# Seams of a two-layer flow-matching backbone: bank order, earlier loads of z's rows, later scaling of rows

## The chip, the cores and the metric

The kernel runs on one core of one Trainium2 chip. The metric is the device time of one execution in microseconds (us). Three runs of the kernel before took 1910.47, 1912.56 and 1915.56, median 1912.56. One more execution was profiled; it took 1914.06, with a span of 1912.3 from its first to its last instruction.

## The reference

Two layers over 512 latent tokens x with a context of 256 tokens, all of width 2048. Each layer normalises its input, scales and shifts it by vectors made from the conditioning (adaLN), mixes the tokens, normalises again, and adds the gated result to the stream.

```python
for i in range(DEPTH):                                   # 2: a pooling layer, then an attention layer
    shift, scale, gate = split(silu(c) @ ada_w[i] + ada_b[i], 3)
    h_lat = rms_norm(x, pre_norm[i]) * (1 + scale) + shift       # the same for the context with c_ctx
    if is_pool:
        u, g = split(h @ w_in, 2)                        # 2048 -> 2 x 2048
        p = centred_multiscale_pool(u)                   # windows 2, 4, 8, 16; minus the token itself
        p = einsum(p, w_grp) + b_grp                     # 4 groups of 512
        y = (p * scale_ * silu(g)) @ w_out               # z = p * scale_ * silu(g); 2048 -> 2048
    else:
        y = mla_branch(h_lat, h_ctx, ...)                # latent attention, 16 heads
    x = x + gate * rms_norm(y, post_norm[i])             # layer 0 also updates the context
return x
```

## The kernel before, in words

Every large product is split for precision: the activation and the weight each consist of a high and a low part, and mm3 (L197) runs three matmuls, L198, L199 and L200, for one product. Weights come in pieces of 128 x 1024: SP's queue loads raw (L186), ScalarE casts the high part whi (L188), VectorE subtracts to get the low part wlo (L189). Two raw and four split buffers rotate. The results stand in eight banks of 512 columns each. pair() alternates between two latent pairs of banks, 0 and 1 or 2 and 3; context results stand in banks 4 and 5. pss() turns between banks 6 and 7, which hold transposes. hss() is bank 7 alone. bank(kind, ...) hands out banks in rotation.

Each engine works through its own list in order. The lists are put in order by a scheduler from the program below; the yields and steps in the program only say which work is issued beside which weight piece. A wait of the first instruction of a list therefore holds up all that stands behind it.

The stages, in the order of time:

- Opening. ada0 makes the scale of layer 0 (rows_, 4 rows in bank 6). part(kts) then turns four of these rows at a time into columns (scales, transposes L371, small VectorE steps up to L387), transposes four column tiles of x through hss() (make_h0: L280, ScalarE L281, VectorE L282), and multiplies each with the first two pairs of w_in's columns, `first` and `second`. rms_rows (L321) makes the row factors of the first norm: it fills ar with the factor of each token (L331), transposes it through hss() (L334) and copies it to R (L335), which has one factor per column, since the products of this stage have channels on the partitions and tokens along the columns. It is called in the last part, before the last lat_part of `second`. ub are two buffers with pads of zeros, in which u_in (L597) puts the scaled products and from which u_out builds the pooled windows.
- Pool layer, first matmul. gemm1 runs pairs j = 2 to 15 of w_in's columns: j below 8 is u, from 8 on the gate. Each takes four pieces (k4) with 16 row tiles. After each piece after(k4) issues other work: fill() gives out steps of ada_part, the conditioning of the later layers as weighted sums on VectorE (L521). At the last pair, j = 15, after(1) and after(2) call load_z for k2 = 0 and 1, that is for four rows of z. Each gate pair ends with its evacuation: VectorE scales by R (L696), ScalarE applies SiLU, VectorE multiplies with y, and GpSimd's queue writes z1d in device memory (L700).
- load_z (L492) reads two rows of z1d back (L496), scales them and splits them into the activation tiles aL (latent) and cbig (context): ScalarE L499, VectorE L500. The first four rows go through the buffer s2, two of them, which also hold y's rows; the other twelve through xt, three of them.
- Pool layer, last matmul for the latents: products(0), four groups of 512 columns, eight pieces each, four latent tiles, one bank per tile and group by bank("l", 1, 8), which starts at bank 0. z_ahead(k2) loads rows 2(k2 + 2) and the next one while the first group runs. Each group is evacuated with a square for the norm (ScalarE L750) and a product with the gate (VectorE L751), into y.
- The same for the context: products(1), with the groups in the order 3, 0, 1, 2 and banks psb() (six, two per group). late=2 lets evacuation lag by two groups. Its tiles y take the place of the latent ones. Beside each piece lat_post(step) moves the latent rows on: residual (L775) takes the norm, adds x (L782), stores to x1d (L785), and scales the rows for the next norm (L794); it is a generator, and every step advances it twice. make_h (L213) then makes the activation of layer 1: four transposes (L220) into a pss() bank, ScalarE L222, a cast L223, VectorE L224. It is done for two row tiles per step, at steps 16 to 23; steps 24 to 31 are those of the fourth context group.
- The attention layer, and its output groups with the last norm: square (L1214), product with the gate (L1215), factor (rms_r, L202: two small VectorE steps L206 and L208, then a power on GpSimd, L210), four final additions (L1245) and stores.

Of the kernel before, what the change touches and what calls it, by code (L numbers as in the profile page):

```python
# [80 lines left out]
def hybrid_kernel(  # L81
# [206 lines left out]
    with pool("start") as sp:  # L288
# [149 lines left out]
        def part(kts):  # L438
# [3 lines left out]
            yield  # L442
            last = kts[-1] == KT - 1
            for i, kt in enumerate((*kts, None)):
                if kt is not None:
                    c_, o = kt // 4, slice(kt % 4 * P, (kt % 4 + 1) * P)
                    make_h0([xs[c_][:, t, o] for t in range(NTL)], kt, 0)
                    yield
                    make_h0([xs[c_][:, t, o] for t in range(NTL, NT)], kt, 1)
                    yield  # L450
                if i >= 1:
                    piece, k = pieces[(i - 1) // 2], kts[i - 1]
                    lat_part(first, piece, k)
                    if not last:
                        cxt_part(first, piece, k)
                    yield
                    if not last:
                        lat_part(second, piece, k)
                    cxt_part(second, piece, k)
                    if last:  # L460
                        cxt_part(first, piece, k)
                    yield
            if last:
                rms_rows()
                for i, kt in enumerate(kts):
                    lat_part(second, pieces[i // 2], kt)
# [101 lines left out]
    with pool("pa") as ap:  # L568
# [25 lines left out]
        for u in ub:  # L594
            nc.gpsimd.memset(u, 0.0)

# [70 lines left out]
        for j in range(2, 2 * NP):  # L667
# [4 lines left out]
            def after(k4):  # L672
                if j <= NP and k4 < 2:
                    u_out((j - 1) // 2, k4, pieces[(j - 1) // 2])
                if j < 2 * NP - 1:
                    fill(1.6 if j < NP else 2.1)
                if j == 2 * NP - 1 and k4 in (1, 2):
                    load_z(lambda: ap.tile([P, ULEN], F32, name="s2", tag="s2", bufs=2), k4 - 1)

# [51 lines left out]
    with pool("pb") as bp:  # L731
# [3 lines left out]
        def h_of():  # L735
            return adp.tile([P, 1024], F32, name="araw", tag="araw", bufs=2)[:, 0:SEQ]

        def products(v, tiles, act_of, before, order, kept, late=0):

# [13 lines left out]
            for n, cc in enumerate(order):  # L753
                waiting.append((cc, gemm_rows(tiles, act_of, pool_w_out[0], cc, before(n), kept if cc == 3 else None,
                                              psb if v else lambda: bank("l", 1, 8))))
                while len(waiting) > (late if n < 3 else 0):
# [18 lines left out]
        def residual(v, t, y, ssq):  # L775
# [13 lines left out]
            r = rms_r(sq, 2, D)  # L789
            yield  # L790
            for half in range(2):
# [5 lines left out]
        def z_ahead(k2):  # L797
            if k2 + 2 < KT // 2:
                load_z(lambda: bp.tile([P, 1024], F32, name="xt", tag="xt", bufs=XTS), k2 + 2)

# [8 lines left out]

        sums_at = lambda: banks[:, (turns["l"] + 3) % 8 * 512:][:, 0:512]  # L810
        ys, ssq = products(0, range(NTL), actl, ahead, (0, 1, 2, 3), kept)
        lat_res = [residual(0, t, ys[t], ssq[t]) for t in range(NTL)]

        def lat_post(step):
            if step >= 20 and len(halves) <= 2 * NTC:
                x_ahead()
            for t in range(NTL):
                if step >= 4 * t:
                    next(lat_res[t], None)
                    next(lat_res[t], None)  # L820
            for kt in range(2 * (step - 16), 2 * (step - 15)):
                if 0 <= kt < KT:
                    make_h(h_of, ys, kt, 1, 0, nc.scalar.copy if kt % 2 else None)
# [369 lines left out]
    with pool("zr_", "right") as zp, pool("pe") as ep:  # L1193
# [15 lines left out]
        for cc in range(4):  # L1209
# [3 lines left out]
            def evac(t, ps):  # L1213
                nc.scalar.activation(junk[:, 0:512], ps, AF.Square, accum_out=ssq[t][:, cc:cc + 1])  # L1214
                nc.vector.tensor_mul(ys[t][:, cc * 512:(cc + 1) * 512], ps, gp)  # L1215

            if cc < 3:
                for t, ps in enumerate(gemm_rows(range(NTL), zzt, wo, cc, load_z2 if cc == 0 else None)):
                    evac(t, ps)
            else:  # L1220
# [14 lines left out]
                for t in range(NTL):  # L1235
# [3 lines left out]
                    for kt in range(KT):  # L1239
                        mm3(ps, zzt(kt, t * P, P), wt(hold[kt // 2], kt % 2, 0, 512), kt == 0, kt == KT - 1)  # L1240
                    evac(t, ps)
                    r = rms_r(ssq[t], 4, D)
                    for q in range(4):
# [28 lines left out]
```

## Time and profile before

| | |
|---|---|
| median of three runs | 1912.56 us (1910.47 to 1915.56) |
| profiled execution | 1914.06 us, of which span 1912.3 |
| busy: TensorE / VectorE / ScalarE / GpSimd | 98% / 64% / 34% / 6% |
| mean granted clock of TensorE | 0.996 of 2.4 GHz |
| 100 to 120: TensorE busy, granted clock | 17.45 of 20 us, 1.00 |
| 120 to 140 | 17.40, 1.00 |
| 680 to 700 | 16.93, 1.00 |
| 700 to 720 | 15.77, 0.91 |
| 880 to 900 | 17.14, 0.91 |
| 940 to 960 | 20.00, 1.00 |

The stretches are counted from the start of the span. TensorE counts as busy while a matmul is in its pipeline, so a stretch at a lower granted clock can be fully busy and still do less. The granted clock is a share of full speed, 1.00 for 2.4 GHz and 0.50 for 1.2 GHz; values between are means over a stretch. In the rows further below, DVE is VectorE, ACT ScalarE, POOL GpSimd, PE TensorE, and SPq the queue of SyncE. In square brackets stands how long an engine was idle before the instruction, and what ended that.

### The profile page before, as it was taken

The numbers are of one execution on the slowest core, as the hardware profiler recorded it, in microseconds if no ns is written. First come the engines' busy times: TensorE is split into PE (matmuls) and PEld (weight loads), VectorE is DVE, ScalarE is ACT, GpSimd is POOL, SyncE is SP. The second block draws the span as 40 slices with busy tenths as digits, with TensorE's granted clock in tenths as the row PEclk, the third lists the DMA queues.
The fourth block names the chain that finished last, engine by engine and source line by source line (L and its number), as shares of the span: only waits on it lengthen the run. The fifth ranks groups of instructions, "written<-read, shape, count | busy, mean of one in ns | idle before, by whom it ended". The sixth has DMA issues, their size and how long they took to land.

```text
span 1912.3 us, 26140 instructions
## 1 busy us (share of the span) xinstructions
PE 1868.5 (98%) x10496; PEld 1618.4 (85%) x10496; DVE 1214.7 (64%) x1572; ACT 643.3 (34%) x1018; POOL 109.3 (6%) x196
## 2 busy tenths in 40 slices
PE   7989999999999989999999999999999999999998
PEld 6778888888888878887889988789999999998886
DVE  6649696885887786575864255635666666664333
ACT  6722121221211234223743232224444444444230
POOL 0000000000100000002010002200000000000000
PEclk9999999999999999999999999999999999999999
DMA  9825454556776676475751237842111112126334
GB/s 312 278 75 179 151 197 134 178 169 197 230 245 214 231 249 226 154 231 208 240 159 50 76 93 266 287 140 91 50 45 50 56 50 67 50 68 189 103 127 154
DMA packets 170442, 299.75 MB, mean 157 GB/s; under 512 B 19624, under 2 KB 89536, under 8 KB 169808
## 3 DMA queue, kind: packets, MB, share of 16 engines
q1 hardware_dynamic: 155136, 243.84, 40.0%
q0 software_dynamic: 13872, 52.07, 7.7%
q10 hardware_dynamic: 1312, 2.16, 0.3%
q8 instruction: 82, 1.34, 0.3%
q14 instruction: 40, 0.33, 0.1%
HBM read 268.65 MB, written 29.38 MB: 156 GB/s over the span
## 4 chain that ended last, share of the span: by engine, by line
PE 83%; DMA 8%; DVE 4%; issue 2%; ACT 2%; POOL 0%; SPq 0%; DVEq 0%; POOLq 0%; ACTq 0%
PE banks L198 25%; PE banks L199 25%; PE banks L200 25%; DMA garaw<-in_ada_w 3%; PE banks L1155 2%; DMA araw<-in_ada_w 1%; PE banks L1134 1%; PE banks L1135 1%; DVE acc L521 1%; DVE wlo L189 1%; PE banks L145 1%; DMA xs<-in_x 1%; DMA raw<-in_ada_w 1%; PE banks L220 1%; DMA s<-z1d 1%
## 5 line engine op out<-in xcount | busy, mean ns | idle before, releaser
L188 ACT CAST whi<-raw 128x1024 fp32r<-128x1024 f32 (+1 forms) x268 | 274.8, 1027 | 670.1 <-PE banks L199 311.0
L189 DVE TENSOR_TENSOR wlo<-raw,whi 128x1024 fp32r<-128x1024 f32 (+1 forms) x268 | 318.8, 1194 | 283.9 <-ACT whi L188 283.0
L521 DVE SCALAR_TENSOR_TENSOR acc<-araw,sc,acc 128x1024 f32<-128x1024 f32 x240 | 297.9, 1280 | 49.4 <-DMA araw<-in_ada_w 48.7
L198 PE MATMUL banks<-aL,whi 128*128 128x512 f32 x704 | 278.1, 395 | 3.5 <-DVE ub L600 2.6
L200 PE MATMUL banks<-aL,wlo 128*128 128x512 f32 x704 | 276.8, 393 | 2.0 <-DVE wlo L189 2.0
L199 PE MATMUL banks<-aL,whi 128*128 128x512 f32 x704 | 276.7, 393 | 0.0
L198 PE MATMUL banks<-whi,aL 128*128 128x512 f32 (+1 forms) x448 | 164.4, 367 | 7.3 <-ACT aL L499 4.2
L198 PE MATMUL banks<-cbig,whi 128*128 128x256 f32 (+2 forms) x576 | 169.8, 295 | 0.9 <-DVE sg L696 0.9
L199 PE MATMUL banks<-cbig,whi 128*128 128x256 f32 (+2 forms) x576 | 170.3, 296 | 0.0
L200 PE MATMUL banks<-cbig,wlo 128*128 128x256 f32 (+2 forms) x576 | 169.1, 293 | 0.0
L199 PE MATMUL banks<-wlo,aL 128*128 128x512 f32 (+1 forms) x448 | 163.7, 365 | 0.0
L200 PE MATMUL banks<-whi,aL 128*128 128x512 f32 (+1 forms) x448 | 162.6, 364 | 0.0
L200 PEld LDWEIGHTS banks<-aL,wlo 128*128 128x128 f32 x704 | 132.6, 188 | 31.7 <-DVE wlo L189 2.9
L198 PEld LDWEIGHTS banks<-aL,whi 128*128 128x128 f32 x704 | 132.8, 189 | 18.0 <-DVE ub L600 3.0
L199 PEld LDWEIGHTS banks<-aL,whi 128*128 128x128 f32 x704 | 133.1, 189 | 13.9
L199 PE MATMUL banks<-wlo,cbig 128*128 128x256 f32 (+2 forms) x384 | 123.6, 322 | 2.9 <-DVE wlo L189 2.9
L198 PE MATMUL banks<-whi,cbig 128*128 128x256 f32 (+2 forms) x384 | 125.1, 326 | 0.1
L198 PEld LDWEIGHTS banks<-cbig,whi 128*128 128x128 f32 x576 | 108.2, 188 | 19.2 <-DVE sg L696 1.2
L200 PE MATMUL banks<-whi,cbig 128*128 128x256 f32 (+2 forms) x384 | 123.6, 322 | 0.0
L199 PEld LDWEIGHTS banks<-cbig,whi 128*128 128x128 f32 x576 | 108.3, 188 | 17.3
L200 PEld LDWEIGHTS banks<-cbig,wlo 128*128 128x128 f32 x576 | 109.3, 190 | 2.9
L1141 ACT ACTIVATE pr<-banks,nm 128x768 f32<-128x768 f32 x64 | 57.8, 903 | 134.1 <-DVE nm L1138 133.9
(258 smaller groups left out, 3567.7 us busy)
## 6 DMA issues: line engine op xcount, KB each, us to landing
araw<-in_ada_w SPq DMA_DIRECT2D x128, 512.0 KB, 4.3
raw<-in_pool_w_in SPq DMA_DIRECT2D x64, 512.0 KB, 4.7
raw<-in_pool_w_out SPq DMA_DIRECT2D x60, 512.0 KB, 5.2
raw<-in_mla_w_in SPq DMA_DIRECT2D x40, 512.0 KB, 4.2
raw<-in_ada_w SPq DMA_DIRECT2D x32, 512.0 KB, 5.8
garaw<-in_ada_w POOLq DMA_DIRECT2D x32, 512.0 KB, 5.5
raw<-in_mla_w_out SPq DMA_DIRECT2D x32, 512.0 KB, 3.9
raw<-in_mla_w_ukv SPq DMA_DIRECT2D x32, 256.0 KB, 3.1
```

The costliest lines, as they stand in the source:

```text
L145: nc.tensor.transpose(pt[:, k * P:(k + 1) * P], acc[:, (lo + k) * P:(lo + k + 1) * P], ident)
L188: nc.scalar.copy(hi[:, :n], raw[:, :n])
L189: nc.vector.tensor_sub(lo[:, :n], raw[:, :n], f32(hi[:, :n]))
L198: nc.tensor.matmul(o, l[0], r[0], start=start, stop=False)
L199: nc.tensor.matmul(o, l[0], r[1], start=False, stop=False)
L200: nc.tensor.matmul(o, l[1], r[0], start=False, stop=stop)
L220: nc.tensor.transpose(pt[:, t * P:(t + 1) * P], xt[:, kt * P:(kt + 1) * P], ident)
L521: nc.vector.scalar_tensor_tensor(acc[v], raw, w, acc[v], ALU.mult, ALU.add)
L1134: nc.tensor.matmul(to, qr[:, o], krh[:, ks], start=True, stop=False)
L1135: nc.tensor.matmul(to, qr[:, o], krl[:, ks], start=False, stop=False)
L1141: nc.scalar.activation(pr, ps[:, 0:KEYS], AF.Exp, bias=nm, accum_out=zs)
L1155: nc.tensor.transpose(pt[:, t * P:(t + 1) * P], pr[:, t * P:(t + 1) * P], ident)
```

## The change

Six edits, at places that lie far apart in the program.

- rms_rows() is called at the start of the last part, behind its scales and the load of its pieces, and no longer near its end.
- ub's tiles are no longer filled whole by GpSimd; VectorE fills the three stretches of pads of each tile.
- In the last gate pair, after(1), after(2) and after(3) load two pairs of z's rows each, twelve rows in all. z_ahead loads the last four, in the first output group.
- Output groups of the latents take banks from a list: the lat pair that the last gate pair did not use, banks 6 and 7, the pair that it used, banks 4 and 5. The sums of the conditioning that still run there use the bank three turns ahead, as before.
- residual yields six times instead of once before it scales the latent rows. make_h follows at steps 18 to 25.
- At the very end the factor's VectorE steps are issued ahead of the last product.

```diff
--- before.py
+++ after.py
@@ -441,6 +441,8 @@
             pieces = [head_piece(kt) for kt in kts[::2]]
             yield
             last = kts[-1] == KT - 1
+            if last:
+                rms_rows()
             for i, kt in enumerate((*kts, None)):
                 if kt is not None:
                     c_, o = kt // 4, slice(kt % 4 * P, (kt % 4 + 1) * P)
@@ -461,7 +463,6 @@
                         cxt_part(first, piece, k)
                     yield
             if last:
-                rms_rows()
                 for i, kt in enumerate(kts):
                     lat_part(second, pieces[i // 2], kt)
 
@@ -592,7 +593,8 @@
 
         ub = [ap.tile([P, ULEN], F32, name=f"ub{k}") for k in range(2)]
         for u in ub:
-            nc.gpsimd.memset(u, 0.0)
+            for lo, n in ((0, PAD), (PAD + SEQ, 2 * PAD), (3 * PAD + KEYS, ULEN - 3 * PAD - KEYS)):
+                nc.vector.memset(u[:, lo:lo + n], 0.0)
 
         def u_in(ps):
             for m, u in enumerate(ub):
@@ -674,8 +676,9 @@
                     u_out((j - 1) // 2, k4, pieces[(j - 1) // 2])
                 if j < 2 * NP - 1:
                     fill(1.6 if j < NP else 2.1)
-                if j == 2 * NP - 1 and k4 in (1, 2):
-                    load_z(lambda: ap.tile([P, ULEN], F32, name="s2", tag="s2", bufs=2), k4 - 1)
+                if j == 2 * NP - 1 and k4:
+                    for k2 in (2 * k4 - 2, 2 * k4 - 1):
+                        load_z(lambda: ap.tile([P, ULEN], F32, name="s2", tag="s2", bufs=2), k2)
 
             ps = gemm1(j * 2 * P, WAYS if j < NP else GATES, after)
             if j < NP:
@@ -735,6 +738,16 @@
         def h_of():
             return adp.tile([P, 1024], F32, name="araw", tag="araw", bufs=2)[:, 0:SEQ]
 
+
+        free = [2 * (1 - ps), 2 * (1 - ps) + 1, 6, 7, 2 * ps, 2 * ps + 1, 4, 5]
+
+        def lbank(ahead=None):
+            i = turns.get("l", 0)
+            if ahead is None:
+                turns["l"] = i + 1
+            at = free[(i + (ahead or 0)) % 8] * 512
+            return banks[:, at:at + 512]
+
         def products(v, tiles, act_of, before, order, kept, late=0):
 
             ys = []
@@ -752,7 +765,7 @@
 
             for n, cc in enumerate(order):
                 waiting.append((cc, gemm_rows(tiles, act_of, pool_w_out[0], cc, before(n), kept if cc == 3 else None,
-                                              psb if v else lambda: bank("l", 1, 8))))
+                                              psb if v else lbank)))
                 while len(waiting) > (late if n < 3 else 0):
                     evac(*waiting.pop(0))
             return ys, ssq
@@ -787,7 +800,8 @@
                     x_ahead()
                 yield
             r = rms_r(sq, 2, D)
-            yield
+            for _ in range(1 if v else 6):
+                yield
             for half in range(2):
                 o = slice(half * 1024, (half + 1) * 1024)
                 with tc.high_priority(offset=-50):
@@ -795,8 +809,8 @@
                 yield
 
         def z_ahead(k2):
-            if k2 + 2 < KT // 2:
-                load_z(lambda: bp.tile([P, 1024], F32, name="xt", tag="xt", bufs=XTS), k2 + 2)
+            if k2 + 6 < KT // 2:
+                load_z(lambda: bp.tile([P, 1024], F32, name="xt", tag="xt", bufs=XTS), k2 + 6)
 
         def ahead(n):
             def step(k2):
@@ -807,7 +821,7 @@
 
         kept = {}
 
-        sums_at = lambda: banks[:, (turns["l"] + 3) % 8 * 512:][:, 0:512]
+        sums_at = lambda: lbank(3)
         ys, ssq = products(0, range(NTL), actl, ahead, (0, 1, 2, 3), kept)
         lat_res = [residual(0, t, ys[t], ssq[t]) for t in range(NTL)]
 
@@ -818,7 +832,7 @@
                 if step >= 4 * t:
                     next(lat_res[t], None)
                     next(lat_res[t], None)
-            for kt in range(2 * (step - 16), 2 * (step - 15)):
+            for kt in range(2 * (step - 18), 2 * (step - 17)):
                 if 0 <= kt < KT:
                     make_h(h_of, ys, kt, 1, 0, nc.scalar.copy if kt % 2 else None)
 
@@ -1212,7 +1226,9 @@
 
             def evac(t, ps):
                 nc.scalar.activation(junk[:, 0:512], ps, AF.Square, accum_out=ssq[t][:, cc:cc + 1])
+                r = rms_r(ssq[t], 4, D) if cc == 3 else None
                 nc.vector.tensor_mul(ys[t][:, cc * 512:(cc + 1) * 512], ps, gp)
+                return r
 
             if cc < 3:
                 for t, ps in enumerate(gemm_rows(range(NTL), zzt, wo, cc, load_z2 if cc == 0 else None)):
@@ -1238,8 +1254,7 @@
                     ps = psb()
                     for kt in range(KT):
                         mm3(ps, zzt(kt, t * P, P), wt(hold[kt // 2], kt % 2, 0, 512), kt == 0, kt == KT - 1)
-                    evac(t, ps)
-                    r = rms_r(ssq[t], 4, D)
+                    r = evac(t, ps)
                     for q in range(4):
                         o = slice(q * 512, (q + 1) * 512)
                         nc.vector.scalar_tensor_tensor(ys[t][:, o], ys[t][:, o], r, xt[:, o], ALU.mult, ALU.add)
```

On TensorE, at the start of the last part of the opening (hwh are weights; xs is x, ar the row factors), before:

```order
L371 MATMUL banks<-ident,ar 128x4 [waits Activation_49]
L371 MATMUL banks<-ident,ar 128x4 x3
L280 MATMUL banks<-ident,xs 128x128 [waits DMAHW6_49,Activation_49]
L280 MATMUL banks<-ident,xs 128x128 x3
L198 MATMUL banks<-aL_103,hwh 128x512 [waits Activation_49]
L198 MATMUL banks<-aL_103,hwh 128x512 x3
L280 MATMUL banks<-ident,xs 128x128 [waits DMAHW7_49,DVE_49]
L280 MATMUL banks<-ident,xs 128x128
```

and now:

```order
L371 MATMUL banks<-ident,ar 128x4 [waits Activation_49]
L371 MATMUL banks<-ident,ar 128x4 x3
L334 MATMUL banks<-ident,ar 128x128 [waits DVE_49,Activation_49]
L334 MATMUL banks<-ident,ar 128x128 x3
L334 MATMUL banks<-ident,ar 128x128 [waits DVE_49]
L334 MATMUL banks<-ident,ar 128x128
L280 MATMUL banks<-ident,xs 128x128 [waits DMAHW6_49,DVE_49]
L280 MATMUL banks<-ident,xs 128x128 x3
L198 MATMUL banks<-aL_103,hwh 128x512 [waits Activation_49]
```

Six transposes of ar stand between the transposes of the scales and those of xs; before, they stand behind the last products of this part.

On VectorE, in the second context group, around the scaling of the first rows of y, before:

```order
L782 SCALAR_TENSOR_TENSOR y<-y,r,xt 128x1024 [waits Pool_49]
L782 SCALAR_TENSOR_TENSOR y<-y,r,xt 128x1024 [waits DMAHW3_49]
L794 TENSOR_SCALAR y<-y,r 128x1024 [waits DMASW5_49]
L794 TENSOR_SCALAR y<-y,r 128x1024 [waits DMASW6_49]
L189 TENSOR_TENSOR wlo<-raw,whi 128x1024 [waits DMAHW0_49,Activation_49]
L206 TENSOR_REDUCE ms<-sq 128x1 [waits Activation_49]
L189 TENSOR_TENSOR wlo<-raw,whi 128x1024 [waits DMAHW1_49,PE_49]
L208 TENSOR_SCALAR ms<-ms 128x1 [waits DVE_49]
L189 TENSOR_TENSOR wlo<-raw,whi 128x1024 [waits DMAHW2_49,Activation_49]
```

and now, where L782 has become L795 and L794 has become L808:

```order
L795 SCALAR_TENSOR_TENSOR y<-y,r,xt 128x1024 [waits Pool_49]
L795 SCALAR_TENSOR_TENSOR y<-y,r,xt 128x1024 [waits DMAHW3_49]
L189 TENSOR_TENSOR wlo<-raw,whi 128x1024 [waits DMAHW0_49,Activation_49]
L189 TENSOR_TENSOR wlo<-raw,whi 128x1024 [waits DMAHW1_49,Activation_49]
L206 TENSOR_REDUCE ms<-sq 128x1 [waits Activation_49]
L808 TENSOR_SCALAR y<-y,r 128x1024 [waits DMASW5_49]
L208 TENSOR_SCALAR ms<-ms 128x1 [waits DVE_49]
L189 TENSOR_TENSOR wlo<-raw,whi 128x1024 [waits DMAHW2_49,Activation_49]
L808 TENSOR_SCALAR y<-y,r 128x1024 [waits DMASW6_49]
L206 TENSOR_REDUCE ms<-ssq 128x1
L808 TENSOR_SCALAR y<-y,r 128x1024 [waits DMASW7_49,Pool_49]
```

The two scalings that wait for the stores of x1d (the semaphores DMASW5 and DMASW6) stood ahead of three weight splits; now two of the splits stand ahead of the first scaling, and one between the two.

On TensorE, at the end of the third context group (y are latent rows, whi and wlo weights, cbig the context), before:

```order
L220 MATMUL banks<-ident,y 128x128 [waits Activation_49]
L220 MATMUL banks<-ident,y 128x128 x3
L220 MATMUL banks<-ident,y 128x128 [waits Activation_49]
L220 MATMUL banks<-ident,y 128x128 x3
L198 MATMUL banks<-whi,cbig 128x512
L199 MATMUL banks<-wlo,cbig 128x512 [waits DVE_49]
L200 MATMUL banks<-whi,cbig 128x512
L198 MATMUL banks<-whi,cbig 128x512
```

and now:

```order
L199 MATMUL banks<-wlo,cbig 128x512
L200 MATMUL banks<-whi,cbig 128x512
L220 MATMUL banks<-ident,y 128x128 [waits Activation_49]
L220 MATMUL banks<-ident,y 128x128 x3
L220 MATMUL banks<-ident,y 128x128 [waits Activation_49]
L220 MATMUL banks<-ident,y 128x128 x3
L220 MATMUL banks<-ident,y 128x128 [waits Activation_49]
L220 MATMUL banks<-ident,y 128x128 x3
L220 MATMUL banks<-ident,y 128x128 [waits Activation_49]
L220 MATMUL banks<-ident,y 128x128 x3
L198 MATMUL banks<-whi,cbig 128x512 [waits DVE_49]
L199 MATMUL banks<-wlo,cbig 128x512
```

Before, the last eight transposes are followed by the last twelve matmuls of the third group, and the first matmul of the fourth group, which waits for VectorE, stands behind those. Now the last sixteen transposes follow each other behind the third group's last matmul, and the waiting matmul stands right behind them.

## Rows read from the trace of the kernel before

**Rows 1.** The page, part 1: busy us (share of span) and instructions.

```profile
PE 1868.5 (98%) x10496; PEld 1618.4 (85%) x10496; DVE 1214.7 (64%) x1572; ACT 643.3 (34%) x1018; POOL 109.3 (6%) x196
```

**Rows 2.** TensorE's waits: line, releaser, total us, times, longest us.

```profile
PE banks L198 <- ACT aL L499: 4.2, 1, 4.2
PE banks L198 <- DVE sg L696: 4.0, 2, 3.1
...
PE banks L199 <- DVE wlo L189: 2.9, 1, 2.9
PE banks L198 <- DVE ub L600: 2.6, 1, 2.6
PE banks L198 <- ACT aL L281: 2.5, 2, 1.8
PE banks L200 <- DVE wlo L189: 2.0, 1, 2.0
```

**Rows 3.** Stretches: length, TensorE busy (instructions), granted clock, DMA share, GB/s.

```profile
690.00:694.00 4.00, 1.76 (x7) 1.00 0.95 305
...
896.00:898.00 2.00, 2.00 (x6) 0.50 0.78 229
...
1234.00:1236.00 2.00, 2.00 (x6) 0.50 1.03 374
```

**Rows 4.** Timeline, last part of the opening: start, length, engine, line, operation [idle before].

```profile
113.97 0.17 DVE L387 SCALAR_TENSOR_TENSOR a<-a,vc 128x8 f32<-128x8 f32 x1
114.97 0.50 PE L198 MATMUL banks<-aL,hwh 128*128 128x512 f32 x1 [1.79 <-ACT aL L281]
...
130.03 0.60 PE L334 MATMUL banks<-ident,ar 128*128 128x128 f32 x4
130.66 0.69 DVE L335 COPY R<-banks 128x512 f32<-128x512 f32 x1
131.89 0.42 DVE L335 COPY R<-banks 128x256 f32<-128x256 f32 x1 [0.53 <-PE banks L334]
```

**Rows 5.** Timeline, GpSimd, the fill of ub.

```profile
136.68 1.49 POOL L595 MEMSET ub<- 128x800 f32 x2
```

**Rows 6.** Timeline, start of the first output group.

```profile
691.41 1.61 DVE L696 TENSOR_TENSOR sg<-banks,R 128x512 f32<-128x512 f32 x3
692.24 0.47 PE L198 MATMUL banks<-whi,aL 128*128 128x512 f32 x1 [3.06 <-DVE sg L696]
```

**Rows 7.** Timeline, SyncE's queue, ScalarE and TensorE: z's rows, and the wait.

```profile
659.34 1.16 SPq L496 DMA_DIRECT2D s<-z1d  x2
666.88 0.33 SPq L496 DMA_DIRECT2D s<-z1d  x1
...
707.03 0.72 ACT L499 ACTIVATE aL<-xt,vc 128x512 fp32r<-128x512 f32 x1 [1.34 <-DMA xt<-z1d]
707.80 0.80 PE L198 MATMUL banks<-whi,aL 128*128 128x512 f32 x1 [4.23 <-ACT aL L499]
...
711.69 0.40 PE L199 MATMUL banks<-wlo,aL 128*128 128x512 f32 x1
711.93 0.40 PE L200 MATMUL banks<-whi,aL 128*128 128x512 f32 x1
```

**Rows 8.** Timeline, VectorE and TensorE, second context group.

```profile
892.26 0.75 DVE L794 TENSOR_SCALAR y<-y,r 128x1024 f32<-128x1024 f32 x1 [3.35 <-DMA x1d<-y]
...
894.20 0.51 PE L199 MATMUL banks<-wlo,cbig 128*128 128x512 f32 x1 [2.86 <-DVE wlo L189]
```

**Rows 9.** Timeline, end of the third context group.

```profile
949.47 1.44 ACT L222 ACTIVATE araw<-banks,s,a 128x512 f32<-128x512 f32 x2
...
951.97 1.03 PE L220 MATMUL banks<-ident,y 128*128 128x128 f32 x8
952.17 1.05 ACT L188 CAST whi<-raw 128x1024 fp32r<-128x1024 f32 x1 [0.60 <-PE banks L200]
952.72 1.29 DVE L751 TENSOR_TENSOR y<-banks,gp 128x512 f32<-128x512 f32 x2 [0.23 <-PE banks L220]
```

## The prediction

> **What bounds the kernel now.** The page's first part comes first: TensorE is busy for 1868.5 of 1912.3 us [rows 1], so a change to the other engines pays only where TensorE stands still, about 44 us in all. The next view is TensorE's waits [rows 2]. It names the instruction that stood still, the instruction that released it, the sum, the count and the longest. Some of the named waits lie in the opening and are untouched here; five of them are the seams that the diff touches: 4.2 us for the first scaled rows of z, 3.1 us for the gate's evacuation (the longest of the two for sg), 2.9 us for a split weight, 2.6 us for ub, and 1.8 us (the longest of two) for a head activation. Together these are 14.6 us. The third view is the granted clock by stretch [rows 3], because a wait has a second price: after the 2.86 us wait for a weight the stretch 896 to 898 runs at 0.50, the lower of the two levels, 1.2 GHz, and holds six matmuls; 1234 to 1236, after a 2.0 us wait, does too. The 3.06 us wait ahead of 692.24 [rows 6] was not followed by a fall: 690 to 694 shows 1.00. So three waits of 2.0 to 4.2 us were followed by half clock and one of 3.1 was not; nor were those of 1.8 and 2.6 (100 to 140 has 1.00 in the table above). I treat it as an even chance per seam.
>
> The price of one fall comes from the wait for z [rows 7]: ten matmuls start between 707.80 and 711.69, 3.89 us, where two later ones start 0.24 apart, so 2.35 us would have done. One fall costs 1.55 us; I use 1.6.
>
> **Part by part.** Minus is time saved.
>
> (a) The row scales (rms_rows, L321) move from behind the last products to the head of the last part. Six transposes, two copies into R and one of the two fills now stand between the scale transposes (L371) and the transposes of x for kt 12, all of them through one bank. In the profile the last small VectorE step of the scales, L387, ends at 114.14 and the first matmul of the part starts at 114.97 [rows 4]. The new order puts behind 114.14: the copy of 512 columns 0.69, a fill of 256 columns (estimate 0.3, below the 0.42 of the copy of that width), two transposes (estimate 0.3 with the handovers, from four in 0.60), the copy of 256 columns 0.42, then four transposes 0.6 and the ScalarE scaling, about 0.72 (two evacuations of that width take 1.44 [rows 9]). That is 3.0 us, so the first matmul starts near 117.2, 2.2 us later. What leaves the end of the part is the transposes' own time there, 0.75 (0.60 for four, and two more after). Net +1.4. Nothing at the end was waiting for R but VectorE's u_in, and that has its own wait (b). Bounds: +0.5, if the copies slip ahead of the 1.2 us weight split that runs on VectorE meanwhile, and +2.2, if the transposes at the end were covered anyway.
>
> (b) ub's fill. GpSimd's fill of both tiles takes 1.49 [rows 5] behind a 0.63 us transfer issue that itself waited for TensorE, and u_in waits for the first half: 0.75 of fill after 136.68, so 137.43. With the pads alone on VectorE six tiny fills replace it, each at most 0.17 like L387 [rows 4], 1.0 in all from about 136.04 on, where GpSimd's issue could start. That is 137.05, a saving of 0.4; at half that price each, 0.9. I take −0.7, with ends −0.4 and −1.4 (fills for nothing).
>
> (c) Banks of the first output group. It now takes the banks of the other pair and the two transposition banks first, so its first matmul no longer waits for L696, which VectorE reaches only at 691.41, behind three accumulations of the next layer's scales. The 3.1 us wait goes. What is late next are those same banks in the second output group, 43 us later by the group's matmuls, so nothing.
>
> (d) z. Twelve instead of four rows are loaded while the last gate pair runs, through the ring s2 with two buffers. Before, the third pair of rows was loaded only at the seam, scaled by ScalarE at 707.03, and TensorE stood for 4.23 until 707.80 [rows 7]; with the fall of the clock, 4.2 + 1.6. Now rows 4 to 11 go in turns of two. One turn lasted from 659.34 to 666.88, 7.5 us. Six turns start by 659.34 + 5 × 7.5 = 697 and are scaled some 9 us later, 706. TensorE, starting the group at about 689.2, needs rows 2k and 2k+1 at 689.2 + 5.5 k (24 matmuls at 0.23 each): 716.6 for rows 10 and 11. Slack 10 us for the last turn; less for the weights, which stand in the same SP queue behind the z loads and are issued between them. Rows 12 to 15 come later through xt, and the last two of them are the product of this very gate pair; its evacuation moves some 3 us back on VectorE, for which I find about 5 us of room. So I take (c) and (d) in full: −3.1 −4.2 −1.6 = −8.9, which is also the best end; the poor end is −3.1, if the wait for z comes back with its fall.
>
> (e) Rows of y are scaled five steps later. Before, L794 stood in VectorE's row until 892.26, 3.35 us for the store of the unscaled rows, and the split behind it released TensorE at 894.20 [rows 8]. In the changed order two weight splits pass ahead of it. Full gain: 2.9 of waiting and one fall of the clock, 1.6, so −4.5. But VectorE and the transfers are crowded in this stretch, and the weights behind come just in time, so some of it is given back on the next pieces; I take −4.0, with ends −1.5 and −4.5.
>
> (f) The new wait. Layer 1's activations (make_h, L213) are made two steps later, 18 instead of 16, so the last four pairs of transposes no longer end one weight piece before the fourth context group but stand right before it. That group needs the banks of the first one, whose evacuation L751 writes tiles that take the place of the latent rows and so waits for the very last transposes. Before, L751 at 952.72 waited 0.23 for them [rows 9] and twelve matmuls, 2.8 us, covered it. Now the two transposition banks turn twice in a row. In the new order ScalarE does, at the end of the third group, a square (about 0.8, estimated from the 0.72 of an evacuation of that width), a weight cast 1.05 and two evacuations, 1.44; the third four transposes wait for the first of these, the fourth for the second. I count from the first transpose. The square starts 0.5 before it, when its bank's last matmul is through, and ends at 0.3; the cast is through at 1.35, the evacuations at 2.07 and 2.8, the last transposes at 3.3, the first L751 (half of 1.29, with a handover) at 4.05. Sixteen transposes in one run would be through in some 1.7, since eight take 1.03 with the end of the last one. So +2.4, with ends +1.0 (the square and the cast already done) and +4.5 (the weight cast waits for its buffer too). Queued behind L751 are the splits of the last activations and two more evacuations; nobody needs those for another 20 us.
>
> (g) The end. Only one small VectorE step passes ahead of the last multiplication, so at most 0.2: −0.1.
>
> The sum without the clock: +1.4 −0.7 −8.9 −4.0 +2.4 −0.1 = −9.9. Seams (a) and (f) now hold 4 us or so without products, and at an even chance of a fall in each one fall is the likeliest count: +1.6. That makes −8.3. Against the profile's own 1914.06 that is 1905.8; the runs' median, 1912.56, is 1.5 lower, so 1904.3 is the forecast.
>
> On the clock the trace says only that some waits of 2 to 4 us are followed by 0.50 and some are not, and that single pairs of transposes between matmuls are followed by 1.00. The Trainium skill (TensorE: Matmul & The Clock Gate, Part 4: PE-mode transpose) says that a transpose "doesn't count as PE-busy the same way" as a matmul. By that rule both seams would fall, since both are stretches of transposes and waits alone, and the sum would be −6.7; no row of this trace holds so many transposes in a row, so it neither agrees nor disagrees.
>
> **Rivals.**
> 1. Both seams (a) and (f) fall to half clock, and (f) costs its upper end: +1.4 + 1.6 and +4.5 + 1.6. For it: three of the waits in the rows of like length fell. Against it: 690 to 694 did not. Sum 3.0 −0.7 −8.9 −4.0 +6.1 −0.1 = −4.6, about 1908.
> 2. (e) doesn't do what it says: the wait for the store leaves the row of the splits but the weights behind are no earlier, and TensorE stops at the next piece for as long. For it: VectorE and the transfers of that stretch are full. Against: the split that was late had its cast ready before. Sum −8.3 + 4.0 = −4.3, about 1908.3.
> 3. The wait for z comes back inside the first output group, once, with its fall: 4.2 + 1.6. For it: rows 12 to 15 depend on the last gate pair through a store and a load, and the weights share SP's queue with twelve loads. Against: 5 to 10 us of room. Sum −2.5, about 1910.
> 4. Slower: the two-buffer ring is the bottleneck. If a turn grows from 7.5 to T, rows 10 and 11 come at 659.34 + 5T + 9 against 716.6. From T = 9.7 on TensorE waits; the saving of 8.3 is eaten at T = 11.3, and at T = 12.5 the kernel is slower by 0.3%. At T = 13 it stands 16.7 us there: −8.3 + 16.7 = +8.4, about 1921. For it: every load in that ring waits for two scalings on VectorE, which also runs the accumulations. Against: the one measured turn is far below it.
>
> **How the numbers follow.** My forecast has 0.66, of which the likeliest is 1904.3 and its own range 1899 to 1907; rival 1 0.10, rival 2 0.09, rival 3 0.09, rival 4 0.06. The low end of the range takes the best ends without a fall: +0.5 −1.4 −8.9 −4.5 +1.0 −0.2 = −13.5, so 1899, and 1 us less for a run's own spread, 1898. The high end takes rival 3, 1910. A measurement of this kernel tells 0.3%, 5.7 us, from no change. The forecast lies on the faster side, rivals 1 and 2 lie within 0.3% but near its edge, and I give a third of them to faster; rival 3 is no change, rival 4 slower: 0.72, 0.22, 0.06.
>
> **What would show it.** In the changed kernel's waits of TensorE the rows for sg, and for L499's aL, should be gone, and the stretch 680 to 720 should gain about 9 us against before. The row for ub should be near 2, and the waits between 112 and 117 together near 4. The wait at 894 should shrink to under 1. A new row should appear: the first matmul of the fourth context group, waiting for y of L764, 1 to 4 us, near 947. The granted clock right behind 117 and behind that new wait decides the 1.6s. The forecast is wrong if a wait for aL or for a split weight stands between 690 and 735, or if the new wait exceeds 5 us.

## The result and the profile after

The changed kernel took 1903.36 us (median of six runs, 1902.64 to 1905.99); the kernel before took 1915.4 beside it (six runs, 1910.47 to 1915.81). The medians differ by 12.0 us. The ratio, which is not their quotient, is 0.9946, with a 95% interval of 0.9933 to 0.9958: about 10 us faster (8.0 to 12.8), and clear of 0.3%. The profiled execution, the slowest of the six, has a span of 1904.2, 8.1 less than before.

TensorE's waits after (line, releaser, total us, times, longest), against [rows 2]:

```profile
PE banks L198 <- DVE sg L699: 1.5, 1, 1.5
...
PE banks L198 <- ACT aL L281: 1.5, 2, 0.8
PE banks L198 <- DVE ub L602: 1.2, 1, 1.2
...
PE banks L199 <- DVE wlo L189: 0.2, 1, 0.2
```

The 4.2 us for z's aL is gone, the wait for sg is no longer the 3.1 us one at the first output group (the 1.5 stands at an earlier gate pair, at 630; before has 0.9 there), the 2.9 us for a split has shrunk to 0.2, and ub's 2.6 to 1.2. New are waits for ar, R, araw and y, which stand in the two timelines below. The stretches (length, TensorE busy and instructions, granted clock, DMA share, GB/s) show the same, with the clock:

```profile
123.00:124.00 1.00, 1.00 (x7) 0.50 0.00 0
124.00:126.00 2.00, 2.00 (x15) 0.84 0.00 0
...
680.00:700.00 20.00, 20.00 (x108) 1.00 0.87 279
700.00:720.00 20.00, 20.00 (x90) 1.00 0.78 243
880.00:900.00 20.00, 20.00 (x88) 1.00 1.01 385
```

The stretch 680 to 720 has no idle time left; it had 16.93 and 15.77 of 20 us. Behind the first seam the clock is at its lower level until about 125, where 100 to 140 had 1.00 before.

Where each product starts tells the seams apart. The table compares the two profiled executions; the last column is what happened since the row above.

| product | before | after | after − before | since the row above |
|---|---|---|---|---|
| first transposes of the last part of the opening | 112.52 | 113.97 | +1.45 | opening, not touched by the edits |
| first product of that part | 114.97 | 118.50 | +3.53 | +2.1 |
| first product that waits for ub | 138.57 | 142.42 | +3.85 | +0.3 |
| first product of the first output group | 692.24 | 693.60 | +1.36 | −2.5 |
| first product of the first context group | 877.01 | 872.10 | −4.91 | −6.3 |
| first product of the fourth context group | 955.61 | 948.55 | −7.06 | −2.2 |
| first product of the last matmul | 1722.70 | 1714.72 | −7.98 | −0.9 |

The first row is no effect of the edits: in the six profiles of kernels that do not have the first two edits, the first transposes of that part start between 112.5 and 114.2.

The first seam, in the timeline (start, length, engine, line, operation, idle before), against [rows 4]:

```profile
113.97 0.66 PE L334 MATMUL banks<-ident,ar 128*128 128x128 f32 x4 [0.76 <-ACT ac L374]
116.11 0.44 PE L334 MATMUL banks<-ident,ar 128*128 128x128 f32 x2 [1.49 <-DVE ar L331]
117.06 0.66 PE L280 MATMUL banks<-ident,xs 128*128 128x128 f32 x4 [0.52 <-DVE R L335]
118.50 2.07 PE L198 MATMUL banks<-aL,hwh 128*128 128x512 f32 x4 [0.78 <-ACT aL L281]
```

And the one at the fourth context group, against [rows 9]:

```profile
944.80 1.04 PE L220 MATMUL banks<-ident,y 128*128 128x128 f32 x8
945.95 1.44 ACT L222 ACTIVATE araw<-banks,s,a 128x512 f32<-128x512 f32 x2
946.77 1.32 PE L220 MATMUL banks<-ident,y 128*128 128x128 f32 x8 [0.94 <-ACT araw L222]
947.81 1.29 DVE L764 TENSOR_TENSOR y<-banks,gp 128x512 f32<-128x512 f32 x2 [0.17 <-PE banks L220]
948.55 0.50 PE L198 MATMUL banks<-whi,cbig 128*128 128x512 f32 x1 [0.46 <-DVE y L764]
```

The transposes wait for ScalarE between their two pairs, and the first product waits for the evacuation that waits for the last of them. At the end of the first seam, VectorE fills ub's pads (0.07 us each) just before u_in:

```profile
141.11 0.32 DVE L597 MEMSET ub<- 128x8 f32 x5 [6.39 <-PE banks L199]
```

### The profile page after: what moved, and what is told of

Read it like the earlier page. It is cut to its first block, busy times and chain, and to the rows that moved or that the text cites. A ratio compares the mean times of both kernels' runs of the same rounds, so it can differ in the third digit from the quotient of the medians.

```text
span 1904.2 us, 26137 instructions
## 1 busy us (share of the span) xinstructions
PE 1867.1 (98%) x10496; PEld 1618.0 (85%) x10496; DVE 1214.6 (64%) x1578; ACT 643.2 (34%) x1018; POOL 108.5 (6%) x194
## 4 chain that ended last, share of the span: by engine, by line
PE 86%; DMA 7%; DVE 3%; issue 2%; ACT 1%; POOL 0%; SPq 0%; DVEq 0%; POOLq 0%; ACTq 0%
PE banks L198 26%; PE banks L199 25%; PE banks L200 25%; DMA garaw<-in_ada_w 3%; PE banks L1169 2%; PE banks L1148 1%; DMA xs<-in_x 1%; PE banks L1149 1%; DMA araw<-in_ada_w 1%; PE banks L145 1%; DMA raw<-in_pool_w_out 1%; PE banks L280 1%; PE banks L362 1%; DVE wlo L189 1%; PE banks L361 1%
```

## The experiments

All ratios are to the kernel before on the same chip, with 95% intervals. Where one kernel is compared with another in microseconds, it is the difference of their ratios times 1915. The experiments ran in three sets of four, each set on its own chip. The changed kernel was not in the first set (the first four below) nor in the last; beside the kernel before it has 0.9946 in the result and 0.9954 in the second set. A difference of less than some 3 us between two kernels is within the intervals.

The profiles differ outside the seams too. From the start of the attention layer to the end, where only the small edit at the very end (g) was made, the fourteen profiles take 929.8 to 934.4 us.

**The early row scales undone** (in the changed kernel):

```diff
-            if last:
-                rms_rows()
             for i, kt in enumerate((*kts, None)):
...
             if last:
+                rms_rows()
                 for i, kt in enumerate(kts):
```

> The changed kernel with one edit undone: rms_rows is called near the end of the last part again, as before. Theory 1, each seam adds by itself: the changed kernel's first products of this part start 2.1 us later than before and then run at half clock until about 125, which costs some 2.5 us, against 0.74 us of transposes saved at the end; undone, the kernel is 3.9 us faster than the changed one (about 1899.5), the wait ahead of the first product of row tile 12 is 1.8 us again and the stretch 118 to 124 shows a granted clock of 1.00. Theory 2, the early row scales are what shortened u_in's wait from 2.6 to 1.2 us: undone, that wait comes back to 2.6 and the gain is only 2.4 us. Theory 3, the fall of the clock was chance: the gain is 1.4 us.

Measured: 1901.65, 0.9924 (0.9912 to 0.9936), 4 to 6 us below the changed kernel's 0.9946 and, in a second set, 0.9954. From the first transposes of the last part to the first product with ub the profile has 114.05 to 138.66, 24.6 us, against 28.45 in the changed kernel: 3.8 less, theory 1's size. One profile without a fall does not tell theory 1 from theory 3, chance; the run of both edits, below, does. Theory 2 falls: ub's wait is 1.16 here too, so the small fills alone made that gain. The clock stayed up at this place:

```profile
118.00:120.00 2.00, 2.00 (x15) 1.00 0.01 4
```

**The early row scales through another bank:**

```diff
-                pt = hss()
+                pt = banks[:, 6 * 512:7 * 512]
```

> The changed kernel with the early row scales kept, but their transposes go through bank 6, which is free by then, and not through bank 7, which the transposes of x use. If sharing bank 7 makes the delay (my theory), the transposes of x no longer wait for the copies into R; what is left is that VectorE does a fill and a copy (0.29 and 0.69) between its small scale steps: the first product starts 1.0 us later than before and not 2.1. With a fall of the clock that is 1.1 us faster than the changed kernel, without one 3.6 us faster (about 1900). If VectorE's own list makes the delay, nothing moves: within 0.5 us of the changed kernel.

Measured: 1900.24, 0.9921 (0.9907 to 0.9936), 5 to 6 us below the changed kernel. The first product starts 3.57 after the first transposes, where the changed kernel takes 4.53 and the old order 2.45. So sharing bank 7 is half of the delay, and VectorE's list the other half, as computed. The clock fell here too (118 to 120 at 0.71, 120 to 122 at 0.50), but for a shorter time. With a fall 1.1 us was expected. From the first transposes to the first product with ub the profile has 26.3 us, 2.2 less than the changed kernel; the rest of the 5 to 6 is not accounted for.

**make_h in six steps:**

```diff
-            for kt in range(2 * (step - 18), 2 * (step - 17)):
+            for kt in range(8 * (step - 18) // 3, 8 * (step - 17) // 3):
```

> The changed kernel, but the sixteen row tiles of make_h are made in steps 18 to 23, two or three per step, so that none is left for the seam to the fourth context group. Theory: the fourth group's 2.2 us of delay go, its first product waits for nothing or up to 0.3 us: 2 us faster than the changed kernel (about 1901.3). Rival: two transposition banks cannot take three row tiles per step, TensorE waits for ScalarE's evacuations within the steps instead, 0.4 us in each of the four steps with three: no gain, or under 0.5 us.

Measured: 1903.49, 0.9937 (0.9922 to 0.9952), 2 to 3 us below the changed kernel by the ratios, though the intervals overlap. TensorE's list of waits has no row between 907 and the attention layer. From the first context group to the attention layer it takes 97.7 us (869.25 to 966.92), the changed kernel 98.8. The rival's waits inside the steps did not appear.

**Both** (the edits of the first and the third experiment):

> Rows back at their old place and make_h in six steps together, all else as in the changed kernel. If the seams add: 3.9 + 2.0 = 5.9 us faster than the changed kernel, about 1897.5, and some 16 us below the kernel before. If a later wait takes the place of what is saved, as the attention layer's waits for split weights near 1218 to 1240 could: 3 us or less.

Measured: 1899.72, 0.9915 (0.9902 to 0.9928): 6 to 7.5 us below the changed kernel, as if the seams added. The profile does not bear that out: 1.3 of its difference from the changed kernel stand at the first seam and 1.2 between the first context group and the attention layer, the rest mostly in the opening (1.4) and in the attention layer (2.5). Its first seam is the old one, with its old 1.79 us wait, and yet the clock fell there:

```profile
118.00:120.00 2.00, 2.00 (x8) 0.50 0.00 0
```

So the fall is not the early row scales' own, as theory 1 had it. From the first transposes to the first product with ub it takes 27.1 us here, with the fall; the changed kernel takes 28.45, 28.46 in its second profile. So the early row scales themselves cost 1.3, near the +1.4 of the sum, and the other 2.5 of the 3.8 above are the fall. In the profiles of all the kernels the old first seam was followed by 0.50 in four of eight (this one and three further below: both edits of z's seam, z's rows alone, rows scaled later alone) and the new one, in its variants, in six of six. A fall at the old one is a matter of chance; whether the longer seam raises the chance, six of six against four of eight does not show.

**Banks alone** (in the kernel before; products() takes lbank and its list, sums_at as in the change):

```diff
-                                              psb if v else lambda: bank("l", 1, 8))))
+                                              psb if v else lbank)))
```

> The kernel before with one edit: output groups of the latents take banks from the changed kernel's list, z's rows are loaded as before. Theory: the two waits at this seam stand in series. TensorE starts the first output group 3.1 us earlier, but rows 4 and up of z are loaded no earlier, so the wait for L499's aL grows from 4.2 to about 7 us: the gain is 0 to 0.5 us. Rival: the waits are independent and the 3.1 us are gained.

Measured: 1915.94, 0.9996 (0.9981 to 1.0012). The wait for sg is gone from the seam and the wait for z has all of it, as the timeline shows:

```profile
707.51 0.79 PE L198 MATMUL banks<-whi,aL 128*128 128x512 f32 x1 [7.39 <-ACT aL L499]
```

3.06 + 4.23 are 7.29 [rows 6, 7].

**z's rows alone:**

```diff
-                if j == 2 * NP - 1 and k4 in (1, 2):
-                    load_z(lambda: ap.tile([P, ULEN], F32, name="s2", tag="s2", bufs=2), k4 - 1)
+                if j == 2 * NP - 1 and k4:
+                    for k2 in (2 * k4 - 2, 2 * k4 - 1):
+                        load_z(lambda: ap.tile([P, ULEN], F32, name="s2", tag="s2", bufs=2), k2)
...
-            if k2 + 2 < KT // 2:
+            if k2 + 6 < KT // 2:
```

> The kernel before with one edit: twelve of z's rows are loaded under the last gate pair, the banks are taken as before. Theory: the wait for L499's aL (4.2) and the fall of the clock behind it (1.6) go, but the gate's evacuation, whose banks the first group still takes, comes later on VectorE behind more of z's scalings, so the wait for sg grows from 3.1 to 5 or 6 us: 3 to 4 us faster than before. Rival: VectorE reaches the evacuation no later, 5.8 us faster.

Measured: 1914.44, 0.9994 (0.9984 to 1.0004), a gain of at most 3 us. The wait for aL is gone and the one for sg grew, but less than I had said, and a fall of the clock followed that one instead:

```profile
695.22 0.50 PE L198 MATMUL banks<-whi,aL 128*128 128x512 f32 x1 [3.48 <-DVE sg L697]
...
695.00:700.00 5.00, 4.78 (x14) 0.66 0.77 250
```

(The second row is of the view of stretches.) In the profile, from ub to the first context group, 733.6 us pass, 4.8 less than before, somewhat more than 3 to 4; the ratio shows 1.1. That profile was the fastest of the kernel's twelve runs, 1908.41 of 1908.41 to 1917.42. Part of what the others lose goes with the clock: the profiled execution has a mean granted clock of 0.997, against 0.996 in the profile of before, while the twelve have 0.9945 on average, against 0.9948 in the runs of the kernel before beside them. Over the runs of either kernel 0.001 of clock goes with 1.2 us, so by this estimate 1.6 of the missing 3.7 us are time at half clock. The rest is open.

**Both edits of that seam:**

> The kernel before with both edits, banks and z's rows. Theory: both waits and the fall go, 8.9 to 9.5 us faster than before, more than the sum of the two edits by themselves (0 to 0.5 and 3 to 4). Rival, a plain sum: what the two give by themselves.

Measured: 1905.51, 0.9944 (0.9931 to 0.9956), 10.7 us below before, where the two alone gave 0.8 and 1.1 by the ratios, both within their intervals of zero. The plain sum of these is refuted. TensorE has no wait after 628.22 and before 887.04.

**The changed kernel again:**

> The changed kernel as it is, on the same chip as the other three, for a comparison of all of them and for a second look at the granted clock behind 118. My theory gives 1 to 2 us more than the kernel with both edits alone saves, 10 to 12 us below the kernel before. If the fall of the clock behind 118 belongs to the early row scales, it is there again; if it is chance, it may be absent, and the time then lies 2.5 us lower.

Measured: 1906.66, 0.9954 (0.9942 to 0.9967), and the fall behind 118 is there again. It is not faster than the two edits alone; by the ratios it is 2 us slower, within the intervals. So the other four edits together gave nothing that these runs can tell from zero. That is no surprise: the prediction's terms for them, +1.4 −0.7 −4.0 +2.4 −0.1 and the fall of 1.6, add up to +0.6.

**Rows scaled later, alone** (make_h at steps 18 to 25 with it):

```diff
             r = rms_r(sq, 2, D)
-            yield
+            for _ in range(1 if v else 6):
+                yield
...
-            for kt in range(2 * (step - 16), 2 * (step - 15)):
+            for kt in range(2 * (step - 18), 2 * (step - 17)):
```

> The kernel before with two edits that belong together: the latent rows are scaled after six yields, and make_h follows at steps 18 to 25. Theory: 4.3 us are won at the second context group (the wait for a split weight and the fall of the clock behind it) and 2.2 us are lost at the fourth, where a first product now waits for the evacuation: 2 us faster than before. Rival: the wait for the split moves on by one or two pieces, then the loss is left: 1 to 2 us slower.

Measured: 1914.12, 0.9993 (0.9982 to 1.0004), 1.3 us. The split's wait at the second context group is gone, the waits at the fourth are there (0.94 and 0.46, as in the changed kernel). From the first context group to the attention layer it takes 98.7 us, 2.2 less than before's 100.9, theory's size; the median cannot tell it from zero.

**The same with make_h in six steps:**

> As the last, but the sixteen row tiles of make_h are made in steps 18 to 23, two or three per step. Theory: the same gain at the second group without the loss at the fourth, 4 us faster than before, 2 us faster than the last. Rival: the gain at the second group is given back.

Measured: 1912.65, 0.9984 (0.9973 to 0.9995). The stretch takes 98.2, 2.7 less than before. The gain of 3 us is in the interval with the expected 4, and 1.7 us better than without the six steps, but the two intervals overlap.

**Six steps and the other bank, in the changed kernel** (the edits of the second and the third experiment):

> The changed kernel with make_h in six steps and with the early row scales through bank 6. If the gains of the two experiments add: 4.8 + 1.7 = 6 us faster than the changed kernel, 0.991 of the kernel before, the same as with rows at their old place and six steps; nothing is left of the delays at either seam but 1 us at the first.

Measured: 1900.87, 0.9924 (0.9912 to 0.9937), 4 to 6 us below the changed kernel, where 6 were expected, and not below the old place of the rows with six steps (0.9915). The profile, of the slowest of its six runs, shows one thing that the expectation did not have:

```profile
908.78 0.50 PE L199 MATMUL banks<-wlo,cbig 128*128 128x512 f32 x1 [2.10 <-DVE wlo L189]
```

In this execution the wait for a split weight came back, some eight pieces later than in [rows 8]. The later scaling of rows leaves the weights just in time, and how much is left of the wait differs by execution: 0.2 in the changed kernel, 0.5 in its second profile, none in the first two experiments, 2.1 here.

**The wait filled with transposes:**

```diff
+        def busy(n):
+            for t in range(n):
+                nc.tensor.transpose(banks[:, 6 * 512 + t % 4 * P:6 * 512 + (t % 4 + 1) * P], ident, ident)
...
                     nc.tensor.transpose(pt[:, t * P:(t + 1) * P], rbv[:, t], ident)
+                busy(14 if lo == 0 else 5)
```

> The changed kernel with 19 idle transposes of the identity into bank 6, which nobody reads, nine ahead of the first four transposes of the row factors and ten behind them. TensorE is then idle for some 1.8 us of that seam and not 3.5, with no product in it still. If transposes count for the clock like products, 118 to 124 shows 1.00 and the kernel is 2 us faster than the changed one; if they do not count, the stretch falls to 0.50 as before and the time is that of the changed kernel or up to 0.5 us more.

In TensorE's list nine of the nineteen stand ahead of the first four transposes of the row factors and ten behind them.

Measured: 1903.37, 0.9935 (0.9922 to 0.9947), 2 to 3.5 us below the changed kernel. The stretches:

```profile
114.00:116.00 2.00, 1.82 (x17) 1.00 0.46 182
116.00:118.00 2.00, 1.09 (x6) 1.00 0.00 0
118.00:120.00 2.00, 1.56 (x5) 0.75 0.00 0
120.00:122.00 2.00, 2.00 (x8) 0.50 0.01 4
122.00:124.00 2.00, 2.00 (x17) 0.90 0.03 8
```

With 1.5 us of idle time in all the clock still fell, behind 5.6 us in which TensorE did nothing but transposes. By itself that would fit the rule of the Trainium skill that I weighed (TensorE: Matmul & The Clock Gate, Part 4: PE-mode transpose). But I had drawn from that rule that both seams fall, and the one at the fourth context group, with sixteen transposes and 1.4 us of waits, was followed by full clock in four of six profiles, the changed kernel's among them. And the old first seam falls in half the profiles without any filling. So the rule is neither shown nor refuted here.

The time was expected to stay and went down, within the intervals. The mean granted clock of the six executions is 0.9977 on average, against 0.9968 in the changed kernel's result and 0.9958 in its second set. At the 1.2 us per 0.001 from above that is 1.1 to 2.3 us, an estimate: over several executions the filled seam may have lost less to the clock than the unfilled one, which one profile with a fall cannot show.

## Why the prediction was right

Forecast 1904.3, measured 1903.36; a saving of 8.3 was forecast, and the profiles differ by 8.1, of which +1.4 is the opening and −0.9 the stretch from the fourth context group to the last matmul, neither touched. The time was met more closely than the saving, and that is luck: the forecast starts from 1912.56, the median of three runs, where six runs have 1915.4. From there a saving of 8.3 would have given 1907.1, and the runs saved about 10 (8.0 to 12.8). The parts by the profile:

(a) The first seam: the first product came 2.1 later, 2.2 was worked out. The links through the shared bank are the ones listed, but the first copy into R, at 115.09, ran ahead of two of the small scale steps and not behind them. The fall of the clock that I gave an even chance came, and cost 2.5 where I had put 1.6, since the lower level lasted to 125: from the first product to the end of the part 22.8 us against 21.0, with 0.75 of transposes gone. That the profile of before had no fall there was a draw too, since the old seam falls in half the profiles.

(b) ub: −1.4 (2.6 to 1.2), where I took −0.7. The best end, fills for nothing, was the right one. The six fills take 0.07 each, where up to 0.17 was put, 0.4 in all, and the first starts before TensorE's last product of the part has ended. The wait of 1.2 that is left is u_in itself; the row for ub had been expected near 2.

(c) and (d): −2.5 and −6.3 by the table, −8.8 together, against −8.9. In (c) the 3.1 went in full; the −2.5 holds a wait for the sg of an earlier gate pair, at 630, that grew by 0.6. The ring of z's rows kept its pace, against rival 4: its six turns of two loads begin at 663.9, 672.0, 677.9, 684.5, 691.4 and 697.8, 6.8 us apart on average where 7.5 was taken. What the experiments add is that the banks' 3.1 us are worth nothing until z's rows come earlier, since the wait behind takes them over in full (7.39 us in the one run), and that both edits together are worth 10.7.

(e) and (f): −2.2 together, against −1.6, in this one pair of profiles. At the end of the third context group the changed kernel is 10.8 ahead (944.56 against 955.38), of which 1.6 are sixteen transposes that it still has to do and 4.9 were there before; that leaves −4.3 for (e), against −4.0. Between there and the fourth group it loses 2.2, against 2.4 worked out. There TensorE waits for araw (0.94) and for y (0.46), 1.4 in all; a single wait for y of 1 to 4 us had been expected. How much of (e) and (f) lasts is less certain: from the first context group to the attention layer the four profiles with the old order take 100.6 to 100.9 us, the six with the changed order 98.4 to 100.6, and the four with make_h in six steps 97.6 to 99.8. By the runs the two edits by themselves are worth 1.3 us, within the interval of zero.

(g): −0.1 was put; from the start of the last matmul on, −8.0 becomes −8.1.

Of the falls of the clock I counted one and one came, at the first seam. The fourth group's seam had no fall in the changed kernel, but two of the six profiles of kernels that have that seam show one (the one with the early row scales undone, 944 to 946 at 0.67, and the one filled with transposes), so that count was a draw. Rival 1, both seams falling, would have given 1908; rivals 2 and 3 did not come, though the 2.1 us wait of one experiment is rival 2 in part.

## What to carry to other kernels

Where two waits stand at one seam, look at what comes behind the first before giving an edit its price. Removing the first alone gave nothing here, since the second grew by as much; removing the second alone gave 4.8 us in one profile and 1.1 (no loss above 0.8, no gain above 3.1) over all runs, the first wait staying, with a fall of the clock behind it; removing both gave 10.7 us. A step that is moved to make room elsewhere takes its buffers with it: both of the losses here, 1.3 us at the first seam (3.8 where only the new seam fell to half clock) and 2.2 at the fourth context group, came from a shared bank or tile that put moved transposes ahead of a waiting product. Leaving the rows where they were and spreading make_h over the steps that were free has the lowest ratio of all that ran, 0.9915; the intervals of the five other variants of the changed kernel (0.9921 to 0.9937) overlap it.

## What the runs showed that I had not expected

The same seam, with the same 1.79 us wait, was followed by half clock in four of eight profiles and by full clock in the others. A single profile therefore cannot show that an edit caused a fall: the one behind the first seam of the changed kernel looked like its price, and half of the profiles without that edit show it too.
